# The convolution's first term on ScalarE, and eight weight tiles' low parts added by DMA, in a gated two-branch layer

## The chip, the cores and the metric

The kernel runs on one core of one Trainium2 chip. The time is the device time of one execution in microseconds (us); a kernel's time is the median of its runs. The profile is of one execution, taken apart from those runs.

The core has engines that run side by side, each with its own in-order queue of instructions: TensorE (PE in the profile; PEld is its weight load), VectorE (DVE), ScalarE (ACT), GpSimd (POOL) and SyncE (SP). Engines wait for one another by semaphores. Transfers (DMAs) are issued by an instruction on one of the queues, here SP's and POOL's, and then run on sixteen DMA engines; a DMA lands when its semaphore says that all its bytes are there.

## The reference

One layer over 512 tokens of 1024 channels. After an RMS norm, one projection makes the inputs of two branches and their gates. The memory branch (mLSTM, four heads of 256, computed in pairs of heads) takes its q and k through a causal convolution of width 4 per channel and a SiLU:

```python
h = rmsnorm(x, norm_w)
proj = jnp.einsum('bsd,de->bse', h, w_in) + b_in
...
qk = jax.nn.silu(causal_depthwise_conv(jnp.concatenate([mq, mk], axis=-1), conv_w, conv_b))
```

so that a channel's value at token t is the sum over j of conv_w[3 - j] x (its projection at t - j, bias included), plus conv_b. The other branch is a stick-breaking attention (eight heads of 128) without softmax. Both are projected, gated, added, sent through an output projection and added to x.

## The kernel before, in words

**Units.** All dense work is cut into units: a weight tile of 128 x 1024 numbers (512 KB), loaded by SP into `stg` (three buffers, tag shared), then split, then multiplied on TensorE. Each operand is held in two parts of the type fp32r, a high part (rounded, `wh`) and a low part (what the rounding left, `wl`), and a product takes three matmuls: high x high, high x low, low x high (`mm3`, L90 to L93). `split` (L95) makes the high part on ScalarE (L96) and the low part by a subtraction on VectorE (L97). A unit has 24 matmuls of 128 x 512, in two halves of twelve. Some units (those of `w_proj_m`, late in the kernel) are marked `by_dma`: there ScalarE makes wh (L123) and writes the same rounded tile with its sign turned into wl (L124), and POOL issues a DMA that adds the original tile from stg to it (L125).

**Order of the units.** Counted from 0: 0 to 15 are q, k, v and the gate of the attention's first four heads, 16 to 31 those of its second four; 32 to 51 are the first memory pair: output gate 32 to 35, gate 36 to 39, q 40 to 43, k 44 to 47, v 48 to 51; 52 to 71 are the second memory pair, with q in 64 to 67 and k in 68 to 71; then the merge gates (72 to 87), the two branch projections (88 to 95 and 96 to 103), and the output projection. The main loop (L1252) goes through the units: at step c it splits the tile of unit c + 2, evacuates unit c - 1 out of PSUM (`evac`), and computes unit c. wh and wl have three buffers each, the dense results four PSUM banks (`psd`); a unit of q, k or a gate takes one bank, and the four v units of a pair take four together, from the first of them on.

**Heads between the halves.** Between the two halves of a unit, each active head advances by one `yield`. The attention's heads 4 to 7 (`SbSet.head`, second set) start at steps 31, 34, 36 and 38. A head splits its q and k (`qtt`, `ktt`; the low parts on VectorE), has TensorE make scores, ScalarE two sigmoids of them (`om`, `a_all`), POOL the causal masks (L466, L469), VectorE the running products (L472, L473) and block transposes into `ay` (L490). Then sixteen DMAs of 40 KB move `ay` into `az` (L509), eight at one step and eight at the next; for these four heads POOL issues them. `az` has two buffers, used by the heads in turn, and a head's az is read in two goes: two pieces (`ath`), and two steps on the last piece (`at`), each split on ScalarE and VectorE.

**The convolution** (`MPair.qk_group`, L701) is the evacuation of the q and k units. ScalarE copies the bank into t and adds the projection's bias (L705); VectorE computes acc = t x w3 + conv_b (L708), then three times acc += t shifted x w (L710); ScalarE takes the sigmoid (L713). The rest of the SiLU (L716), the high part (L721) and the low part (L725) of a unit are interleaved with the next unit's evacuation by `self.prev`. acc has one buffer.

POOL's DMAs use eight semaphores in rotation; each waits for the previous transfer on its semaphore.

Of the kernel before, what the change touches and what calls it, by code (L numbers as in the profile page):

```python
# [11 lines left out]
AF = mybir.ActivationFunctionType  # L12
OP = mybir.AluOpType
# [22 lines left out]
def tile_hybrid_layer(  # L36
# [16 lines left out]
    nc = tc.nc  # L53
# [20 lines left out]
    def blk(tag, dt=F32, shape=(512,), name=None, p=128):  # L74

        where = mp if tag in MISC else sp
        return where.tile([p] + list(shape), dt, name=name or tag, tag=tag, bufs=BUFS[tag])

    def two(tag, dt=F32, name=None):

        t = blk(tag, dt, (2, 512), name=name)
        return t[:, 0, :], t[:, 1, :]

    def dense_ps():
        return psd.tile([128, 512], F32, name="dps", tag="dps")

    def att_ps():
        return psa.tile([128, 512], F32, name="aps", tag="aps")

    def mm3(ps, ah, al, bh, bl, first, last):  # L90
        nc.tensor.matmul(ps, ah, bh, start=first, stop=False)  # L91
        nc.tensor.matmul(ps, ah, bl, start=False, stop=False)  # L92
        nc.tensor.matmul(ps, al, bh, start=False, stop=last)  # L93
# [6 lines left out]
    class Unit:  # L100


        def __init__(self, src, c0, rows=None):
            if rows is None:
                self.ap = src[:, c0:c0 + 128].rearrange("(k p) c -> p k c", p=128)
                self.shape = [KT, 128]
            else:
                self.ap = src[rows:rows + 256, c0:c0 + 512].rearrange("(k p) c -> p k c", p=128)
                self.shape = [2, 512]
            self.slow = None  # L110
            self.heavy = False
            self.by_dma = False
# [16 lines left out]
    units = []  # L129

    def chan_group(src, c0, n, mov, evac, slow=None):
        for ct in range(n // 128):
            u = Unit(src, c0 + 128 * ct)

            def mm(half, u=u, ct=ct):
                if half == 0:
                    u.ps = dense_ps()
                for k in range(4 * half, 4 * half + 4):
                    mh, ml = mov(k)
                    mm3(u.ps, u.wh[:, k, :], u.wl[:, k, :], mh, ml, k == 0, k == KT - 1)  # L140

            u.mm = mm
            u.evac = lambda u=u, ct=ct: evac(ct, u.ps)
            u.slow = slow
            units.append(u)
# [50 lines left out]
    def defer(n, fn):  # L196
        later.setdefault(now[0] + n, []).append(fn)
# [24 lines left out]
    vec = cst.tile([128, 98], F32, name="vec")  # L222
    bvec = cst.tile([128, 56], F32, name="bvec")
# [23 lines left out]
    def turn_vecs():  # L247
        vp = att_ps()
        nc.tensor.transpose(vp[:, 0:98], v_rows, ident[0:98, 0:98])
        nc.tensor.transpose(vp[:, 98:154], b_rows, ident[0:56, 0:56])  # L250
        nc.vector.tensor_copy(vec, vp[:, 0:98])
        nc.vector.tensor_copy(bvec, vp[:, 98:154])
        nc.vector.scalar_tensor_tensor(qkw, vec[:, 96:97], 128 ** -0.5, vec[:, 97:98],
                                       op0=OP.mult, op1=OP.mult)

    def cw(j, ct):
        return vec[:, 8 + 16 * j + ct:9 + 16 * j + ct]

    def cb(ct):
        return vec[:, 72 + ct:73 + ct]  # L260
# [4 lines left out]
    def bias(ct):  # L265
        return bvec[:, ct:ct + 1]
# [51 lines left out]
    class SbSet:  # L318
# [95 lines left out]
        def v_group(self):  # L414
            row = []

            def evac(tb, ps):
                t = blk("tmp")
                nc.vector.tensor_tensor(t, ps, row[0], op=OP.add)
                vh = blk("vh", FR, (576,))[:, 0:512]  # L420
                vl = blk("vl", FR)
                nc.scalar.activation(vh, t, AF.Copy)
                self.v.append((vh, vl))
                if tb == TB - 1:
                    done.add(("v", self.s))
                return lambda: nc.vector.tensor_tensor(vl, t, vh.bitcast(F32), op=OP.subtract)

            tok_group(w_in, C_SV + 512 * self.s, h_sta, evac, False, C_SV + 512 * self.s, row)
# [246 lines left out]
    class MPair:  # L675
        def __init__(self, p):
            self.p = p
            self.prev = lambda: None
            self.tr = {"q": [], "k": []}
            self.v = []  # L680

# [19 lines left out]
        def qk_group(self, name, c0, o):  # L701
            def evac(ct, ps):
                ch = o + 4 * self.p + ct
                t = blk("tmp")
                nc.scalar.activation(t, ps, AF.Identity, bias=bias(ch))  # L705
                self.prev()
                acc = blk("acc")
                nc.vector.tensor_scalar(acc, t, cw(3, ch), cb(ch), op0=OP.mult, op1=OP.add)  # L708
                for j in (1, 2, 3):
                    nc.vector.scalar_tensor_tensor(acc[:, j:], t[:, 0:T - j], cw(3 - j, ch), acc[:, j:],  # L710
                                                   op0=OP.mult, op1=OP.add)
                self.prev()
                nc.scalar.activation(t, acc, AF.Sigmoid)  # L713

                def mult():
                    nc.vector.scalar_tensor_tensor(t, acc, 1.0 if name == "q" else 0.0625, t,  # L716
                                                   op0=OP.mult, op1=OP.mult)

                    def high():
                        th, tl = two("qk", FR, name="m%st" % name)  # L720
                        nc.scalar.activation(th, t, AF.Copy)  # L721
                        self.tr[name].append((th, tl))

                        def low():
                            nc.vector.tensor_tensor(tl, t, th.bitcast(F32), op=OP.subtract)  # L725
                            if ct == 3:
                                done.add(("m" + name, self.p))
                        self.prev = low
                    self.prev = high

                self.prev = mult
                if ct == 3 and name == "k":
                    def flush():
                        for _ in range(3):
                            self.prev()
                        self.prev = lambda: None
                    defer(1, flush)

            chan_group(w_in, c0 + 512 * self.p, 512, h_mov, evac, lambda: self.prev())

        def v_group(self):
            row = []
# [127 lines left out]
    pairs = [MPair(0), MPair(1)]  # L870
# [103 lines left out]

    chan_group(w_proj_m, 0, D, lambda k: ymp[k], pm_evac)
    n_proj = len(units)
    for un in units[n_proj - 8:]:
        un.by_dma = True


# [230 lines left out]
    for tb in range(TB):  # L1211
        units[tb].mm = first_mm(tb)

    later.setdefault(3, []).append(turn_vecs)
    later.setdefault(GATES_PREP, []).append(gates_prep)

# [102 lines left out]
```

## Time and profile before

| | us |
|---|---|
| Time, median of 3 runs | 705.88 (705.53 to 706.02) |
| The profiled execution's own time | 706.65 |
| Its span, first to last instruction | 704.9 |
| TensorE busy in it | 691.1 |
| VectorE, ScalarE, POOL busy | 472.4, 334.9, 166.0 |
| Units 40 to 47 on TensorE | 265.72 to 314.96 |
| Mean granted TensorE clock | 0.994 |

Rows of the timeline read: start, duration, engine, line, operation, written tile <- read tiles, shape, count, and in brackets the idle time just before and what ended it. Durations of neighbours on one engine overlap by a tenth or so in the rows: the spacing of starts is what an operation costs on its engine. Times are from the start of the span.

### The profile page before, as it was taken

How to read it: one execution, taken by the hardware profiler on the slowest of the kernel's cores; microseconds unless marked ns; L12 is line 12 of the kernel's file. 1: busy time of each engine (PE TensorE's matmuls, PEld its weight loads, DVE VectorE, ACT ScalarE, POOL GpSimd, SP SyncE). 2: the span in 40 equal slices, each digit the busy share in tenths (PEclk: the TensorE clock that was granted, in tenths of full speed). 3: DMA queues.
4: the chain of work that ended last, by engine and by line, in shares of the span. 5: the costliest groups of instructions: out<-in, count | busy, mean ns of one | idle time of the engine just before them, and what ended most of it. 6: DMA issues, size and time to landing. Idle time of an engine off the chain costs nothing.

```text
span 704.9 us, 9367 instructions
## 1 busy us (share of the span) xinstructions
PE 691.1 (98%) x3172; PEld 574.0 (81%) x3172; DVE 472.4 (67%) x835; ACT 334.9 (48%) x629; POOL 166.0 (24%) x361
## 2 busy tenths in 40 slices
PE   8999999999999999997999999999999999999997
PEld 6888788888888888885888888888888888888885
DVE  6847987866836897898634638995444364446995
ACT  6245364575335663444365634446463353344451
POOL 5422122265831686040002020001111000111010
PEclk9999999999999999998999999999999999999999
DMA  7423524525653443342332234433323456589344
GB/s 244 136 87 102 170 63 125 143 78 154 181 141 91 113 111 94 95 127 75 89 95 86 60 100 128 118 90 89 90 61 83 114 161 211 155 176 215 111 90 120
DMA packets 109113, 84.11 MB, mean 119 GB/s; under 512 B 8302, under 2 KB 91656, under 8 KB 109064
## 3 DMA queue, kind: packets, MB, share of 16 engines
q1 hardware_dynamic: 103320, 73.40, 36.4%
q0 software_dynamic: 5600, 9.97, 6.5%
q8 instruction: 25, 0.41, 0.2%
q14 instruction: 24, 0.20, 0.1%
q10 hardware_dynamic: 144, 0.13, 0.1%
HBM read 65.12 MB, written 2.10 MB: 95 GB/s over the span
## 4 chain that ended last, share of the span: by engine, by line
PE 59%; issue 12%; DVE 9%; DMA 6%; POOL 3%; ACT 1%; SPq 0%; DVEq 0%; POOLq 0%; ACTq 0%
PE dps L91 17%; PE dps L93 17%; PE dps L92 17%; DVE acc L710 2%; DMA wl<-stg 2%; POOL az L509 2%; PE aps L92 2%; PE aps L93 2%; PE aps L91 2%; DVE wl L97 1%; DMA az<-ay 1%; DMA xr<-u 1%; DMA stg<-in_w_proj_m_dram 1%; DMA xr<-in_x_dram 1%; DVE om L472 1%
## 5 line engine op out<-in xcount | busy, mean ns | idle before, releaser
L97 DVE TENSOR_TENSOR wl<-stg,wh 128x1024 fp32r<-128x1024 f32 x92 | 112.5, 1223 | 116.5 <-ACT wh L96 115.4
L91 PE MATMUL dps<-hh,wh 128*128 128x512 f32 x448 | 175.1, 391 | 0.0
L93 PE MATMUL dps<-hh,wl 128*128 128x512 f32 x448 | 174.5, 390 | 0.0
L92 PE MATMUL dps<-hl,wh 128*128 128x512 f32 x448 | 174.4, 389 | 0.0
L96 ACT ACTIVATE wh<-stg 128x1024 fp32r<-128x1024 f32 x92 | 96.8, 1052 | 64.5 <-PE dps L93 39.8
L93 PEld LDWEIGHTS dps<-hh,wl 128*128 128x128 f32 x448 | 84.1, 188 | 17.9
L92 PEld LDWEIGHTS dps<-hl,wh 128*128 128x128 f32 x448 | 84.2, 188 | 16.7
L91 PEld LDWEIGHTS dps<-hh,wh 128*128 128x128 f32 x448 | 84.2, 188 | 16.5
L91 PE MATMUL dps<-wh,hh 128*128 128x512 f32 x224 | 89.3, 399 | 4.8 <-ACT tmp L705 4.4
L93 PE MATMUL dps<-wh,hl 128*128 128x512 f32 x224 | 88.3, 394 | 0.0
L92 PE MATMUL dps<-wl,hh 128*128 128x512 f32 x224 | 88.2, 394 | 0.0
L91 PEld LDWEIGHTS dps<-wh,hh 128*128 128x128 f32 x224 | 42.8, 191 | 14.2 <-ACT tmp L705 4.8
L93 PEld LDWEIGHTS dps<-wh,hl 128*128 128x128 f32 x224 | 42.6, 190 | 9.2
L92 PEld LDWEIGHTS dps<-wl,hh 128*128 128x128 f32 x224 | 42.7, 191 | 8.4
L509 POOL DMA_DIRECT2D az<-ay x64 | 32.1, 508 | 25.0 <-DVE at L97 24.1
L713 ACT ACTIVATE tmp<-acc 128x512 f32<-128x512 f32 x16 | 10.1, 633 | 57.3 <-DVE acc L710 57.3
L710 DVE SCALAR_TENSOR_TENSOR acc<-tmp,vec,acc 128x511 f32<-128x511 f32 (+2 forms) x48 | 36.0, 750 | 1.7
L466 POOL TENSOR_SCALAR_AFFINE_SELECT om<-om 128x128 f32<-128x128 f32 x32 | 17.3, 541 | 80.0 <-ACT om L464 80.0
L472 DVE TENSOR_TENSOR_SCAN om<-om 128x512 f32<-128x512 f32 (+3 forms) x32 | 26.7, 834 | 8.6 <-POOL om L466 8.6
L125 POOL DMA_DIRECT2D wl<-stg x8 | 7.0, 870 | 93.7 <-DVE yml L97 61.7
L464 ACT ACTIVATE om<-aps,rq 128x512 f32<-128x512 f32 (+3 forms) x32 | 16.8, 526 | 21.6 <-PE aps L93 21.6
L399 POOL DMA_DIRECT2D tz<-ty x48 | 25.9, 549 | 5.0 <-DVE ty L389 2.4
(284 smaller groups left out, 1273.8 us busy)
## 6 DMA issues: line engine op xcount, KB each, us to landing
stg<-in_w_in_dram SPq DMA_DIRECT2D x87, 512.0 KB, 4.0
stg<-in_w_proj_s_dram SPq DMA_DIRECT2D x8, 512.0 KB, 3.9
B<-in_w_out_dram SPq DMA_DIRECT2D x8, 512.0 KB, 4.8
stg<-in_w_proj_m_dram SPq DMA_DIRECT2D x8, 512.0 KB, 3.7
wl<-stg POOLq DMA_DIRECT2D x8, 512.0 KB, 5.5
az<-ay SPq DMA_DIRECT2D x64, 40.0 KB, 2.7
az<-ay POOLq DMA_DIRECT2D x64, 40.0 KB, 2.0
brow<-in_b_in_dram SPq DMA_DIRECT2D x8, 256.0 KB, 5.5
```

What stands on the lines that cost most here:

```text
L91: nc.tensor.matmul(ps, ah, bh, start=first, stop=False)
L92: nc.tensor.matmul(ps, ah, bl, start=False, stop=False)
L93: nc.tensor.matmul(ps, al, bh, start=False, stop=last)
L96: nc.scalar.activation(hi, src, AF.Copy)
L97: nc.vector.tensor_tensor(lo, src, hi.bitcast(F32), op=OP.subtract)
L399: q.dma_start(tz[32 * b:32 * b + 32, :, a, :], src[32 * a:32 * a + 32, b])
L464: nc.scalar.activation(om[:, 0:n], zp, AF.Sigmoid, scale=rn[:, h:h + 1])
L466: nc.gpsimd.affine_select(out=om[:, ts], in_=om[:, ts], compare_op=OP.is_gt, fill=1.0, base=0, channel_multiplier=1, pattern=[[-1, 128]])
L472: nc.vector.tensor_tensor_scan(back, back, back, 1.0, op0=OP.mult, op1=OP.bypass)
L509: q.dma_start(az[32 * a:32 * a + 32, b, :, :], ay[32 * b:32 * b + 32, a, :, :])
L710: nc.vector.scalar_tensor_tensor(acc[:, j:], t[:, 0:T - j], cw(3 - j, ch), acc[:, j:], op0=OP.mult, op1=OP.add)
L713: nc.scalar.activation(t, acc, AF.Sigmoid)
```

## The change

Three things are done. The first term of the convolution, acc = t x w3 + conv_b on VectorE, becomes a second pass of ScalarE over the same PSUM bank, acc = ps x w3 + b'. As ps lacks the projection's bias, b' = w3 x bias + conv_b takes the place of conv_b; it is made once in the setup, by two small VectorE operations on 128 x 16 numbers; t and the other three terms stay as they were. And the eight q and k units of the first memory pair (40 to 47) are marked `by_dma`, as those of `w_proj_m` were before. Those of the second pair (64 to 71) get the new first term alone.

```diff
--- before.py
+++ after.py
@@ -250,6 +250,9 @@
         nc.tensor.transpose(vp[:, 98:154], b_rows, ident[0:56, 0:56])
         nc.vector.tensor_copy(vec, vp[:, 0:98])
         nc.vector.tensor_copy(bvec, vp[:, 98:154])
+
+        nc.vector.tensor_tensor(vp[:, 160:176], vec[:, 56:72], bvec[:, 0:16], op=OP.mult)
+        nc.vector.tensor_tensor(vec[:, 72:88], vp[:, 160:176], vec[:, 72:88], op=OP.add)
         nc.vector.scalar_tensor_tensor(qkw, vec[:, 96:97], 128 ** -0.5, vec[:, 97:98],
                                        op0=OP.mult, op1=OP.mult)
 
@@ -676,6 +679,7 @@
         def __init__(self, p):
             self.p = p
             self.prev = lambda: None
+            self.dense = []
             self.tr = {"q": [], "k": []}
             self.v = []
 
@@ -705,7 +709,7 @@
                 nc.scalar.activation(t, ps, AF.Identity, bias=bias(ch))
                 self.prev()
                 acc = blk("acc")
-                nc.vector.tensor_scalar(acc, t, cw(3, ch), cb(ch), op0=OP.mult, op1=OP.add)
+                nc.scalar.activation(acc, ps, AF.Identity, scale=cw(3, ch), bias=cb(ch))
                 for j in (1, 2, 3):
                     nc.vector.scalar_tensor_tensor(acc[:, j:], t[:, 0:T - j], cw(3 - j, ch), acc[:, j:],
                                                    op0=OP.mult, op1=OP.add)
@@ -737,6 +741,7 @@
                     defer(1, flush)
 
             chan_group(w_in, c0 + 512 * self.p, 512, h_mov, evac, lambda: self.prev())
+            self.dense.extend(units[-4:])
 
         def v_group(self):
             row = []
@@ -974,7 +979,7 @@
 
     chan_group(w_proj_m, 0, D, lambda k: ymp[k], pm_evac)
     n_proj = len(units)
-    for un in units[n_proj - 8:]:
+    for un in units[n_proj - 8:] + sum([p.dense for p in pairs[:1]], []):
         un.by_dma = True
```

In the changed kernel the lines are shifted: L705 becomes L709, L708 L712, L710 L714, L713 L717, L509 L512; L123 to L125 stay.

## The prediction

> **What bounds the kernel now.** I read the busy shares first, then what TensorE waited for, then the chain that ended last, then the four engines' timelines where that chain leaves TensorE.
>
> ```profile
> PE 691.1 (98%) x3172; PEld 574.0 (81%) x3172; DVE 472.4 (67%) x835; ACT 334.9 (48%) x629; POOL 166.0 (24%) x361
> PE dps L91 <- ACT tmp L705: 4.4, 1, 4.4
> PE aps L92 <- DVE ktt L97: 0.4, 1, 0.4
> 325.53 0.68 ACT tmp L705
> 326.25 0.79 PE dps L91
> ...
> 331.31 0.42 PE dps L93
> 331.73 0.24 PE dps L91
> 326.25 0.79 PE L91 MATMUL dps<-wh,hh 128*128 128x512 f32 x1 [4.42 <-ACT tmp L705]
> 291.24 0.39 PE L91 MATMUL dps<-hh,wh 128*128 128x512 f32 x1
> 296.68 0.39 PE L91 MATMUL dps<-hh,wh 128*128 128x512 f32 x1
> ```
>
> The first line has each engine's busy time; the next two are from the list of TensorE's waits (for whom: total, times, longest); then come pieces of the chain, and from TensorE's timeline the matmul behind the wait and the first ones of units 44 and 45. TensorE is busy all the time and sets the end. (Units are weight tiles, counted from 0; 40 to 43 are q and 44 to 47 are k of the first memory pair.) Its one long wait, 4.42 us before 326.25, is for L705: the four PSUM banks are full, and ScalarE is late emptying the one of unit 47. Behind the wait the matmuls start 0.43 apart instead of 0.227 (unit 44's 24 take 296.68 - 291.24 = 5.44): twelve take 326.25 to 331.73, 5.48 us, against 2.72, so 2.75 more. What can be won at TensorE here is 4.42 + 2.75 = 7.17 us.
>
> The lateness comes from VectorE's pace:
>
> ```profile
> 302.44 2.32 DVE L710 SCALAR_TENSOR_TENSOR acc<-tmp,vec,acc 128x511 f32<-128x511 f32 x3
> 306.47 1.22 DVE L97 TENSOR_TENSOR wl<-stg,wh 128x1024 fp32r<-128x1024 f32 x1 [0.26 <-ACT wh L96]
> 307.61 0.54 DVE L708 TENSOR_SCALAR acc<-tmp,vec 128x512 f32<-128x512 f32 x1
> 308.19 2.32 DVE L710 SCALAR_TENSOR_TENSOR acc<-tmp,vec,acc 128x511 f32<-128x511 f32 x3
> 304.85 0.63 ACT L713 ACTIVATE tmp<-acc 128x512 f32<-128x512 f32 x1 [3.38 <-DVE acc L710]
> 305.39 1.05 ACT L96 ACTIVATE wh<-stg 128x1024 fp32r<-128x1024 f32 x1
> 306.34 0.67 ACT L705 ACTIVATE tmp<-dps,bvec 128x512 f32<-128x512 f32 x1
> 306.91 0.62 ACT L721 ACTIVATE mqt<-tmp 128x512 fp32r<-128x512 f32 x1
> ```
>
> One round of the convolution (a unit's evacuation) takes 308.19 - 302.44 = 5.75 us, and VectorE has hardly a gap in it; a unit without head work takes 5.44 on TensorE, so each round falls behind a little, and rounds with a head's splits in them more. ScalarE, in the second half of the rows, waits 3.38 of each round for VectorE.
>
> **The change part by part.** It takes from VectorE, per unit of the first pair, the low part (1.14, from 306.47 to 307.61) and the first term (0.58). ScalarE gets them: a second 128x1024 copy (0.95) and a 128x512 pass from PSUM (0.57, as L705). A round becomes a loop through ScalarE: sigmoid 0.54, wh 0.95, wl 0.95, L705 0.57, high part 0.57, first term 0.57, handover 0.1, three VectorE terms and handover 2.41 (302.44 to 304.85): 6.66 us, 0.9 longer than now. So VectorE is relieved and the round isn't shorter. In the second pair, without the copy, it is 5.71, about today's pace: nothing there. The two small setup operations cost as this one, off the path:
>
> ```profile
> L252 DVE COPY bvec<-aps x1: 206/206/206, 36.5 to 36.5; 128x56 f32<-128x56 f32 x1
> ```
>
> That is 0.4 us at most (around 36.5 us, where TensorE's list names no wait for a low part), and I count 0.
>
> What decides is POOL's queue: the low part is now issued there, among the stick-breaking heads' copies az<-ay (heads 4 to 7, eight copies at a time). POOL, before, at units 38 and 39:
>
> ```order
> L509 DMA az_2731<-ay_2580 32x320 x8
> L465 MEMSET om_2750 128x1
> L466 AFFINE_SELECT om_2750<-om_2750 128x128
> L469 AFFINE_SELECT a_all_2664<-a_all_2664 128x128
> L465 MEMSET om_2760 128x1
> ```
>
> The same place after, with the semaphores waited for:
>
> ```order
> L125 DMA wl_2715<-stg_2558 128x1024 [waits DMASW0_49,DMAHW2_49,PE_49,Activation_49]
> L512 DMA az_2734<-ay_2582 32x320 [waits DMAHW4_49,DMAHW3_49,DMAHW5_49,DMAHW1_49,DMAHW6_49,DMAHW0_49,DMAHW7_49,DMASW1_49,DVE_49]
> L512 DMA az_2734<-ay_2582 32x320 [waits DMASW2_49]
> L512 DMA az_2734<-ay_2582 32x320 [waits DMASW3_49]
> L512 DMA az_2734<-ay_2582 32x320 [waits DMASW4_49]
> L512 DMA az_2734<-ay_2582 32x320 [waits DMASW5_49]
> L512 DMA az_2734<-ay_2582 32x320 [waits DMASW6_49]
> L512 DMA az_2734<-ay_2582 32x320 [waits DMASW7_49]
> L512 DMA az_2734<-ay_2582 32x320 [waits DMASW0_49]
> L468 MEMSET om_2753 128x1
> L469 AFFINE_SELECT om_2753<-om_2753 128x128 [waits Activation_49]
> ```
>
> A low part moved in ahead of the copies. Each DMA of POOL takes the next of eight semaphores and waits for that one's previous transfer. The low part has semaphore 0, so the eighth copy waits until the low part has landed; behind it stand the masks of head 7 (AFFINE_SELECT), behind those VectorE's scans, and behind these on VectorE the low parts qtt and ktt that the next scores need. Three units on, POOL before:
>
> ```order
> L465 MEMSET om_2938 128x1
> L466 AFFINE_SELECT om_2938<-om_2938 128x128
> L469 AFFINE_SELECT a_all_2832<-a_all_2832 128x128
> L509 DMA az_2909<-ay_2740 32x320 x8
> L509 DMA az_3058<-ay_2918 32x320 x16
> L751 MEMSET vh_3513 128x2
> ```
>
> and after:
>
> ```order
> L512 DMA az_2914<-ay_2743 32x320 x8
> L125 DMA wl_3034<-stg_2889 128x1024
> L512 DMA az_3065<-ay_2923 32x320 x8
> L125 DMA wl_3088<-stg_2970 128x1024
> L512 DMA az_3065<-ay_2923 32x320 x8
> L125 DMA wl_3158<-stg_3038 128x1024
> L125 DMA wl_3202<-stg_3092 128x1024
> ```
>
> wl_3034 is unit 44's low part and wl_3088 unit 45's, which now stands behind head 7's first eight copies. What these wait for, and the prices of the walk:
>
> ```profile
> 251.79 3.94 POOL L509 DMA_DIRECT2D az<-ay  x8 [0.36 <-DVE ay L490]
> 272.46 3.94 POOL L509 DMA_DIRECT2D az<-ay  x8 [6.57 <-DVE at L97]
> 299.38 6.55 POOL L509 DMA_DIRECT2D az<-ay  x13 [17.51 <-DVE at L97]
> 306.50 1.76 POOL L509 DMA_DIRECT2D az<-ay  x3 [0.57 <-DMA az<-ay]
> 298.52 0.56 DVE L97 TENSOR_TENSOR at<-az,at 128x384 fp32r<-128x384 f32 x1 [0.57 <-ACT at L96]
> 253.01 1.05 ACT L96 ACTIVATE wh<-stg 128x1024 fp32r<-128x1024 f32 x1
> 618.42 1.04 ACT L124 ACTIVATE wl<-stg 128x1024 fp32r<-128x1024 f32 x1
> 619.75 0.86 POOL L125 DMA_DIRECT2D wl<-stg  x1 [4.57 <-ACT wl L124]
> DMA to landing us min/median/max: 4.6/5.5/8.2
> 257.73 0.65 DVE L472 TENSOR_TENSOR_SCAN om<-om 128x256 f32<-128x256 f32 x1
> 261.70 0.50 PE L92 MATMUL aps<-ktt,qtt 128*128 128x512 f32 x1 [0.37 <-DVE ktt L97]
> 265.72 0.39 PE L91 MATMUL dps<-hh,wh 128*128 128x512 f32 x1
> 276.78 0.76 DVE L472 TENSOR_TENSOR_SCAN om<-om 128x256 f32<-128x256 f32 x1 [3.62 <-POOL om L466]
> 279.61 1.22 DVE L97 TENSOR_TENSOR wl<-stg,wh 128x1024 fp32r<-128x1024 f32 x1
> 284.56 0.39 PE L91 MATMUL dps<-hh,wh 128*128 128x512 f32 x1
> 297.99 0.51 ACT L96 ACTIVATE at<-az 128x384 fp32r<-128x384 f32 x1
> 298.40 1.03 ACT L96 ACTIVATE ath<-az 128x512 fp32r<-128x512 f32 x2
> ```
>
> Head 7's copies start at 299.38, 0.3 after head 5's last split (298.52 + 0.56) frees the two-buffer tile az; head 6's wait likewise (272.46). They issue eight in 3.94. The landing row is of the eight low parts that are made by DMA today, late in the kernel.
>
> The walk, from these durations. (a) Unit 40: wl on ScalarE from 253.96, POOL issues at 255.3 (0.29 after its end, as 618.42 to 619.75), landing at 255.3 + 5.5 = 260.8; the eighth copy 0.49, its mask 0.38 (276.78 - 272.46 - 3.94): first scan at 261.7, not 257.73. From that scan to the scoring matmul that waits for ktt are 3.97 today: 265.65, 3.95 later than 261.70. The idle of 0.37 + 3.95 = 4.3 is as long as the 4.42 above, so I add its 2.75 of clock; unit 40 starts at 272.4.
> (b) ScalarE then empties unit 39 (0.6), makes wh and wl (1.9) and head 4's piece (0.41, 297.99 to 298.40): 275.3; VectorE's split 0.65, POOL 0.3: copies from 276.3. Unit 42's low part, issued at 275.2, lands at 280.7; with the last copy and mask 281.6. Scans as from 276.78 to 279.61, 2.83: the three terms of unit 40 start at 284.4, its sigmoid 2.41 later at 286.8.
> (c) Two rounds, 6.66 + 1.03 (ath) and 6.66: sigmoid of unit 42 at 301.15; it takes 0.54, head 5's piece 0.41, VectorE 0.65, POOL 0.3: head 7's copies at 303.05; eight of them, 3.94: unit 45's low part is issued at 307.0 and lands at 312.5.
> (d) TensorE reaches unit 45 at 272.4 + (296.68 - 265.72) = 303.4 and its third matmul, the first with wl, 0.45 later. It waits 8.7, and the clock costs 2.75 again; unit 45 ends at 312.5 + 22 x 0.227 + 2.75 = 320.3. The low parts of 40 to 44 come in time (44, the closest, at 296.1 for 298.3); that of 46, behind eight more copies and the landing of 45, comes at 318.5, before 320.3.
> (e) Rounds 43 and 44 end at about 316, before unit 45 does, so the lag is gone by then. The first term keeps a bank 1.14 longer (high part and its own pass), which matters only where banks are short, at unit 48, and not without the lag. So the old wait goes, with its clock: 7.17.
> (f) SP's loads into stg now wait for a landing in place of VectorE. That of unit 48 starts at 312.5 and takes the page's 4.0 us, to 316.5; ScalarE can split it only when unit 45 frees its wh, at 320.3. It is hidden, by 3.8 (the row, and those on the landing, stand here):
>
> ```profile
> stg<-in_w_in_dram SPq DMA_DIRECT2D x87, 512.0 KB, 4.0
> 250.00:300.00 50.00, 49.63 (x227) 41.23 (x226) 43.28 (x81) 24.01 (x43) 24.07 (x57) 1.00 0.36 101
> 600.00:650.00 50.00, 50.00 (x222) 41.41 (x221) 25.38 (x38) 20.79 (x24) 6.96 (x8) 1.00 0.78 183
> q0 software_dynamic: 1054, 3.86, 42.1%
> ```
>
> Sum: 3.95 + 2.75 + 8.7 + 2.75 - 7.17 = +11.0. The profiled execution took 706.65 (span 704.9), 0.77 above the median 705.88: 717.65, or 716.9 on the median's scale. Differences under 0.2% (1.4 us) I call none.
>
> Two prices have no row at this place. The landing has 4.6 to 8.2 late in the kernel; I take its 5.5, because the traffic will be alike: the DMA share is 0.36 in 250 to 300 and 0.78 in 600 to 650 (the number before the last), where POOL's own eight low parts are 42.1% of the queues' time, and 0.36 + 0.42 = 0.78. Three landings lie on the path (units 40, 42, 45): -2.7 if all take 4.6, +5.4 if two take 8.2. The clock after (a) is bounded by 0 (the wait of 0.37 was followed by no halving) and 2.75; I take the near row. [...]
>
> **The rivals.**
> Forecast (74%): waits as walked; with those bounds 711.5 to 722.3.
> Least wait (12%): (a) doesn't reach TensorE and nothing runs late. Even so, from unit 42's end to unit 45's landing are 6.12 (the loop without its sigmoid) + 0.54 + 0.41 + 0.65 + 0.3 + 3.94 + 5.5 = 17.5, against 296.68 - 284.56 + 0.45 = 12.6 until the need: 4.9 + 2.75 - 7.17 = +0.5, 706.4. That is no measurable change. Against it: VectorE waits for POOL's masks even today (3.62 at 276.78).
> Faster (14%): head 7's copies wait only for their own transposes, and POOL comes to unit 45 at once. It decides at a landing by 297.1, an issue by 291.6. Then only relief is left: -7.17, 698.7. For it: VectorE loses 1.7 of 5.75 per unit. Against it: the 17.51 row, and the order.
>
> **How the numbers follow.** 716.9 is the likeliest. 706 to 722.5 takes in the forecast's bounds and the least wait, and leaves out the faster case and about 0.06 at the forecast's ends. Least wait counts mostly as none: faster 0.14, same 0.08, slower 0.78.
>
> **What would show it.** Right: PE waits for ktt (about 4 us near 262) and for a DMA wl at unit 45 (about 9), each with a halved clock; the L705 wait gone; VectorE's share down, gaps before its scans. Wrong: no PE wait for wl, or POOL issuing unit 45's low part before 292.

## The result, and the profile after

| | before | after |
|---|---|---|
| Median (lowest to highest) | 705.95 us (705.53 to 706.37), 4 runs | 714.54 us (714.12 to 715.41), 4 runs |
| The profiled execution's own time, its span | 706.65, 704.9 | 714.22, 712.5 |

The ratio is 1.0123, with a 95% interval from 1.0106 to 1.0141: 8.6 us slower. The busy times of the engines, and the head of the list of TensorE's waits, after:

```profile
PE 690.1 (97%) x3172; PEld 573.2 (80%) x3172; DVE 456.7 (64%) x813; ACT 353.2 (50%) x653; POOL 170.7 (24%) x369
```

```profile
PE dps L93 <- DMA wl<-stg: 8.7, 1, 8.7
PE aps L92 <- DVE ktt L97: 4.3, 1, 4.3
```

The change did what it says: VectorE has 15.7 us less, ScalarE 18.3 more. The old wait for L705 isn't in the list any more; in its place stand two, one for a low part that a DMA makes and one for ktt. POOL's timeline shows where both come from:

```profile
254.60 0.94 POOL L125 DMA_DIRECT2D wl<-stg  x1 [3.91 <-ACT wl L124]
255.41 3.59 POOL L512 DMA_DIRECT2D az<-ay  x7
259.77 0.50 POOL L512 DMA_DIRECT2D az<-ay  x1 [0.76 <-DMA wl<-stg]
...
303.00 3.95 POOL L512 DMA_DIRECT2D az<-ay  x8 [11.69 <-DVE at L97]
306.91 0.98 POOL L125 DMA_DIRECT2D wl<-stg  x1
```

The first row is unit 40's low part. The first seven copies stand behind it, so they start at 255.41 where they started at 251.79 before; the eighth waits 0.76 more for its landing. (Row times count from the start of each span. Unit 36 starts 0.71 us sooner in this execution than in the one before, so on a common clock the seven copies are 4.33 late.) The last two rows are head 7's copies, held 11.69 us for the end of head 5's splits, and behind them unit 45's low part. VectorE, with the scan that needs the mask and the first convolution terms of unit 40:

```profile
260.64 0.84 DVE L475 TENSOR_TENSOR_SCAN om<-om 128x256 f32<-128x256 f32 x1 [4.80 <-POOL om L469]
...
264.14 0.69 DVE L97 TENSOR_TENSOR ktt<-tz,ktt 128x512 fp32r<-128x512 f32 x1
...
284.21 2.31 DVE L714 SCALAR_TENSOR_TENSOR acc<-tmp,vec,acc 128x511 f32<-128x511 f32 x3
```

ScalarE's sigmoids of units 40 to 42, and its wait before them, which ends with VectorE's terms:

```profile
286.62 0.63 ACT L717 ACTIVATE tmp<-acc 128x512 f32<-128x512 f32 x1 [4.75 <-DVE acc L714]
...
294.32 0.64 ACT L717 ACTIVATE tmp<-acc 128x512 f32<-128x512 f32 x1 [2.45 <-DVE acc L714]
...
301.06 0.63 ACT L717 ACTIVATE tmp<-acc 128x512 f32<-128x512 f32 x1 [2.45 <-DVE acc L714]
```

And TensorE at the two waits (302.39 is unit 45's first matmul, 311.74 the first that needs its wl):

```profile
264.89 0.79 PE L92 MATMUL aps<-ktt,qtt 128*128 128x512 f32 x1 [4.27 <-DVE ktt L97]
...
302.39 0.39 PE L91 MATMUL dps<-hh,wh 128*128 128x512 f32 x1
302.61 0.39 PE L92 MATMUL dps<-hl,wh 128*128 128x512 f32 x1
311.74 0.80 PE L93 MATMUL dps<-hh,wl 128*128 128x512 f32 x1 [8.74 <-DMA wl<-stg]
312.34 0.63 PE L91 MATMUL dps<-hh,wh 128*128 128x512 f32 x1
...
314.47 0.50 PE L93 MATMUL dps<-hh,wl 128*128 128x512 f32 x1
314.81 0.39 PE L91 MATMUL dps<-hh,wh 128*128 128x512 f32 x1
```

To compare kernels, this table gives where units start on TensorE, in us after unit 36, whose surroundings are alike in all of them; then where unit 36 itself starts, and how long the rest from unit 104 to the end of the span takes. All are starts of first matmuls in the timelines of the profiled executions.

| kernel | 40 | 45 | 46 | 48 | 50 | 104 | unit 36 at | 104 to end |
|---|---|---|---|---|---|---|---|---|
| before | 26.33 | 57.29 | 62.73 | 75.57 | 96.30 | 421.61 | 239.39 | 43.90 |
| after | 32.72 | 63.71 | 79.53 | 92.41 | 105.25 | 430.56 | 238.68 | 43.26 |
| term_only | 26.33 | 57.29 | 62.73 | 75.57 | 95.07 | 420.38 | 240.65 | 43.97 |
| dma_only | 32.74 | 63.70 | 79.59 | 92.70 | 105.54 | 430.85 | 238.67 | 43.48 |
| own_az | 31.82 | 62.79 | 68.23 | 82.57 | 102.32 | 427.63 | 239.12 | 42.65 |
| from_42 | 26.31 | 57.27 | 73.05 | 85.91 | 98.75 | 424.08 | 238.81 | 47.51 |
| both_mends | 26.30 | 57.26 | 62.70 | 77.16 | 95.64 | 421.16 | 238.58 | 46.16 |
| tiny_dma | 26.31 | 57.27 | 62.71 | 77.21 | 95.52 | 420.83 | 239.49 | 42.78 |
| act_load | 26.34 | 57.30 | 62.74 | 75.91 | 97.84 | 423.57 | 238.88 | 43.95 |
| shadow_before | 26.30 | 57.25 | 62.69 | 76.64 | 90.36 | 415.66 | 238.87 | 43.87 |
| shadow_term | 26.32 | 57.28 | 63.18 | 79.67 | 95.39 | 420.77 | 239.04 | 43.99 |
| shadow_after | 32.43 | 64.91 | 78.79 | 92.12 | 104.96 | 430.54 | 238.37 | 43.09 |
| shadow_dma | 26.35 | 58.97 | 65.48 | 80.57 | 93.41 | 418.72 | 238.34 | 42.74 |

After, TensorE loses 32.72 - 26.33 = 6.39 at unit 40 and (79.53 - 63.71) - (62.73 - 57.29) = 10.38 at unit 45, and wins (96.30 - 75.57) - (105.25 - 92.41) = 7.89 at unit 48. From unit 50 to unit 104 both kernels take 325.31, so nothing more happens there.

### The profile page after: what moved, and what is told of

It reads as the page before. It is cut to its first block, busy times and chain, and to the rows that moved or that the text cites. A ratio compares the mean times of both kernels' runs of the same rounds, so it can differ in the third digit from the quotient of the medians.

```text
span 712.5 us, 9379 instructions
## 1 busy us (share of the span) xinstructions
PE 690.1 (97%) x3172; PEld 573.2 (80%) x3172; DVE 456.7 (64%) x813; ACT 353.2 (50%) x653; POOL 170.7 (24%) x369
## 4 chain that ended last, share of the span: by engine, by line
PE 79%; DMA 4%; DVE 3%; issue 2%; ACT 2%; POOL 1%; SPq 0%; DVEq 0%; ACTq 0%; POOLq 0%
PE dps L91 23%; PE dps L93 23%; PE dps L92 23%; PE aps L92 3%; PE aps L93 3%; PE aps L91 3%; DMA wl<-stg 2%; DMA az<-ay 1%; PE aps L823 1%; PE aps L825 1%; PE aps L824 1%; DVE acc L714 1%; DMA stg<-in_w_in_dram 1%; POOL az L512 1%; SPq L512 0%
## 5 line engine op out<-in xcount | busy, mean ns | idle before, releaser
L97 DVE TENSOR_TENSOR wl<-stg,wh 128x1024 fp32r<-128x1024 f32 x84 | 102.6, 1222 | 120.3 <-ACT wh L96 119.2
L96 ACT ACTIVATE wh<-stg 128x1024 fp32r<-128x1024 f32 x84 | 88.4, 1053 | 66.5 <-PE dps L93 41.6
L714 DVE SCALAR_TENSOR_TENSOR acc<-tmp,vec,acc 128x511 f32<-128x511 f32 (+2 forms) x48 | 36.0, 750 | 15.4 <-ACT acc L712 14.3
L125 POOL DMA_DIRECT2D wl<-stg x16 | 14.3, 916 | 106.2 <-DVE yml L97 61.7
L512 POOL DMA_DIRECT2D az<-ay x64 | 32.8, 638 | 16.0 <-DVE at L97 11.7
L469 POOL TENSOR_SCALAR_AFFINE_SELECT om<-om 128x128 f32<-128x128 f32 x32 | 15.8, 494 | 79.4 <-ACT om L467 79.4
L717 ACT ACTIVATE tmp<-acc 128x512 f32<-128x512 f32 x16 | 10.1, 633 | 41.5 <-DVE acc L714 41.5
L123 ACT ACTIVATE wh<-stg 128x1024 fp32r<-128x1024 f32 x16 | 16.9, 1055 | 26.8 <-PE dps L92 20.4
L467 ACT ACTIVATE om<-aps,rq 128x512 f32<-128x512 f32 (+3 forms) x32 | 16.8, 525 | 23.4 <-PE aps L93 23.3
```

The costliest lines, as they stand in the source:

```text
L96: nc.scalar.activation(hi, src, AF.Copy)
L97: nc.vector.tensor_tensor(lo, src, hi.bitcast(F32), op=OP.subtract)
L123: nc.scalar.activation(self.wh, self.st, AF.Copy)
L125: nc.gpsimd.dma_start(out=self.wl, in_=self.st, accum_op=OP.add)
L467: nc.scalar.activation(om[:, 0:n], zp, AF.Sigmoid, scale=rn[:, h:h + 1])
L469: nc.gpsimd.affine_select(out=om[:, ts], in_=om[:, ts], compare_op=OP.is_gt, fill=1.0, base=0, channel_multiplier=1, pattern=[[-1, 128]])
```

## The experiments

My theory was the prediction's: POOL's queue, in two places that are independent of each other. The rivals were that one of the two parts of the change costs by itself what it puts on ScalarE, and that the waits only move.

**The first term alone** (term_only). The changed kernel without the marks:

```diff
-    for un in units[n_proj - 8:] + sum([p.dense for p in pairs[:1]], []):
+    for un in units[n_proj - 8:]:
```

> The changed kernel with the low parts of units 40 to 47 back on VectorE: only the first term of the convolution moves to ScalarE. Theory (the loss comes from POOL's queue): both new waits of TensorE, for ktt and for unit 45's low part, are gone; a round of the convolution is a loop through ScalarE of 5.7 us, so VectorE's relief of 0.58 counts only in the three rounds that also hold a head's splits, about 1.7 us; 704.2, with a rest of the wait for a bank at unit 48. Rival (the loss comes from ScalarE's added passes in the round): slower than before, about 708.

Measured: 705.26 us, ratio 0.9998 (0.9988 to 1.0007) to the kernel before. TensorE's longest wait:

```profile
PE dps L91 <- ACT acc L712: 4.5, 2, 4.1
```

No change that can be measured, where I had expected 704.2; the bank wait at unit 48 stays and is now ended by the new pass L712. In this execution unit 50 comes 1.2 us sooner (95.07 for 96.30), but the wait itself is only 0.29 shorter (4.13 for 4.42). The rest is TensorE's clock, which stood at half for 3.42 us of the work behind the wait in place of 5.34 (see point (d) below on how that comes about).

**The low parts alone** (dma_only): the first term back on VectorE, the marks kept.

```diff
-                nc.scalar.activation(acc, ps, AF.Identity, scale=cw(3, ch), bias=cb(ch))
+                nc.vector.tensor_scalar(acc, t, cw(3, ch), cb(ch), op0=OP.mult, op1=OP.add)
```

(and the two setup operations that fold the bias are taken out).

> The changed kernel with the first term back on VectorE: only the low parts of units 40 to 47 go by DMA. Theory (POOL's queue): nearly the whole loss stays; the wait for ktt (about 4 us and its clock) as it is, the wait at unit 45 about 1 us shorter, since a round has one ScalarE pass and the high part less in its loop (6.1 for 6.7): 713.4. Rival (ScalarE's added passes): half of the loss, about 710.

Measured: 714.77 us, 1.0125 (1.0105 to 1.0146), with waits of 8.8 for the DMA and 4.2 for ktt. The whole loss lies in the low parts; the first term doesn't add to it. I had expected a wait 1 us shorter at unit 45, and it isn't: head 7's copies go out 0.7 us sooner (302.31) and the low part 0.4 sooner (306.47), but this one takes 5.2 us to land, for 4.8.

**Head 7's copies in other buffers** (own_az): the changed kernel, where head 7's az comes from a tag of four buffers, so its copies need not wait for head 5's splits.

```diff
-            az = sp.tile([128, 4, 10, 32], F32, name="az", tag="P5", bufs=2)
+            last = self.s and h == 3
+            az = sp.tile([128, 4, 10, 32], F32, name="az", tag="A" if last else "P5", bufs=4 if last else 2)
```

> The changed kernel, but head 7's az is taken from the four-buffer tag A, so that its copies need not wait until head 5's last split has freed the two-buffer tag P5. Nothing else is moved. Theory (unit 45's low part stands behind copies that wait): TensorE's wait of 8.7 us at unit 45 is gone. But the rounds, now 6.7 us, are late all the same, and TensorE no longer stands still for them: the old wait for a bank at unit 48 is back with 4 to 5 us and its clock. The two nearly cancel: about 712. Rival (the DMA itself is too slow, or the sixteen DMA engines too full): the wait at unit 45 stays, 714.5.

Measured: 710.78 us, 1.0076 (1.0059 to 1.0093). POOL's rows for head 7's first copies and unit 45's low part, and TensorE's waits:

```profile
290.44 3.78 POOL L513 DMA_DIRECT2D az<-ay  x7
...
296.61 0.92 POOL L125 DMA_DIRECT2D wl<-stg  x1 [1.12 <-ACT wl L124]
```

```profile
PE aps L92 <- DVE ktt L97: 4.3, 1, 4.3
PE dps L91 <- ACT acc L713: 3.8, 1, 3.8
PE dps L93 <- DMA wl<-stg: 1.2, 1, 1.2
```

The copies go out 12.6 us sooner, the low part 10.3 sooner, and the wait of 8.7 falls to 1.2. At once the bank wait at unit 48 is back. So the second wait is the copies' wait for az, and part of what it costs in the changed kernel is offset by the old wait that it hides.

**Units 40 and 41 split as before** (from_42):

```diff
-    for un in units[n_proj - 8:] + sum([p.dense for p in pairs[:1]], []):
+    for un in units[n_proj - 8:] + pairs[0].dense[2:]:
```

> The changed kernel, but units 40 and 41 are split by VectorE; 42 to 47 go by DMA. Theory: no low part stands ahead of the copies and masks of steps 38 and 39, so the wait for ktt and its clock (6.4 us) are gone. Unit 45's low part still waits for head 5's last split, and TensorE reaches unit 45 6.4 us sooner while that split comes about 3 us sooner, so that wait grows to about 12: about 712. Rival (each low part by DMA costs about the same, 1.1 us of the 8.6 for each of eight): 712.4 too, but with both waits shortened in proportion instead of one gone and one longer.

Measured: 712.44 us, 1.0097 (1.0082 to 1.0112). POOL's rows:

```profile
251.20 3.93 POOL L512 DMA_DIRECT2D az<-ay  x8 [0.37 <-DVE ay L493]
...
296.66 3.95 POOL L512 DMA_DIRECT2D az<-ay  x8 [11.69 <-DVE at L97]
300.59 0.97 POOL L125 DMA_DIRECT2D wl<-stg  x1
...
687.63 1.77 POOL L1092 DMA_DIRECT2D xr<-u  x2 [13.78 <-DVE wl L97]
```

The eight copies of the first row start as in the kernel before, and the wait for ktt is gone: unit 40 starts at 26.31, as before the change. The wait at unit 45 stays, 8.7; I had thought that it would grow to 12. It doesn't, because head 7's copies too go out 6.34 us sooner (296.66 for 303.00), by as much as TensorE reaches unit 45 sooner (57.27 for 63.71), and not 3. In the stretch this kernel is only 98.75 - 96.30 = 2.45 late, yet its median is 6.9 above. Most of the rest is at the other end of the kernel (47.51 us from unit 104, for 43.90), and the last row belongs to it: an accumulating DMA of the output projection waits for a VectorE operation later than its source u, and later TensorE waits 1.8 for the wl of the last unit. The kernel before, at the same place, and then the changed kernel one pair of these DMAs earlier:

```profile
682.79 1.75 POOL L1087 DMA_DIRECT2D xr<-u  x2 [10.86 <-DVE u L1104]
```

```profile
681.36 1.75 POOL L1092 DMA_DIRECT2D xr<-u  x2 [25.25 <-DVE wl L97]
```

Such a wait stands in the changed kernel too, at the first pair, and its end is no longer than before (43.26). So the wait alone doesn't make the end longer; where it falls matters.

**Both mends** (both_mends): the two edits above together.

> The changed kernel with units 40 and 41 split by VectorE as before and with head 7's copies in buffers of their own; units 42 to 47 still get their low parts by accumulating DMA. Theory (the loss is two waits of POOL's queue, each with a place of its own): no wait for ktt above 0.5 us, a wait of at most 3 us for a low part at unit 45 (it was 1.2 with the own buffers alone), the bank wait at unit 48 back at 3.5 to 7 us; unit 50 starts 0 to 2 us later after unit 36 than in the kernel before; 706 to 708 us, plus the 3.5 us at the end of the kernel that the run with units 40 and 41 alone changed showed, should it come from the number of POOL's DMAs, which is the same here. Rival (the 0.95 us more of ScalarE's work per unit is what costs): the stretch is no shorter than with either mend alone, unit 50 is 5 us or more late, 711 us or more.

Measured: 707.89 us (705.78 to 709.48), 1.0036 (1.0023 to 1.0048). In the stretch unit 50 is 0.66 earlier than before the change, with waits of 3.7 for a bank and 1.3 for a low part. The two losses are independent: counted at unit 50, the own buffers alone win 2.93, the split of units 40 and 41 alone 6.50, and both together 9.61, about the sum of the two and more than the 8.95 that the change loses there. The longer end is there again, 46.16.

**Two small DMAs** (tiny_dma): both mends, and for units 40 and 41 a DMA of 512 bytes where the changed kernel issues the low part.

```diff
                 split(self.st, self.wh, self.wl)
+                if self in pairs[0].dense[:2]:
+                    nc.gpsimd.dma_start(out=sp.tile([128, 1], F32, name="nul", tag="nul", bufs=1), in_=vec[:, 0:1])
```

> Both mends, and on POOL, in the places where the changed kernel issues the low parts of units 40 and 41, a DMA of 512 bytes each into a tile that nothing reads: as many POOL DMAs as the changed kernel has, each on the same one of the eight semaphores. Theory (the eighth copy of head 5 waits for the landing of what holds its semaphore, and what matters is that 512 KB land late; the longer end of the kernel with six DMAs more comes from the semaphores that its last DMAs then get): no wait for ktt above 0.6 us; no wait for wl at unit 107; 42.6 to 44.0 us from unit 104 to the end in place of 46.2 and 47.5; 704 to 706 us. Rival (the longer end has another cause): it stays at 46 us or more, 707.9 us.

Measured: 704.16 us (702.67 to 704.80, 7 runs), 0.9975 (0.9964 to 0.9986). POOL:

```profile
251.49 0.57 POOL L129 DMA_DIRECT2D nul<-vec  x1
252.06 3.94 POOL L515 DMA_DIRECT2D az<-ay  x8
...
682.51 1.77 POOL L1095 DMA_DIRECT2D xr<-u  x2 [8.30 <-DVE u L1112]
```

The DMA ahead of the copies costs TensorE nothing here: it has no wait before it, it takes POOL 0.57 us, the eight copies behind it take 3.94 as before, and unit 40 starts at 26.31. And the end is 42.78 again. With 0 or 8 POOL DMAs more than before it took 42.65 to 43.99 in all kernels of the table, with 6 more 46.16 and 47.51. As POOL's DMAs take eight semaphores in turn, the number of DMAs ahead, modulo eight, sets which semaphores the last ones get, and that fits these three counts; other counts were not run. Why it makes one of the last DMAs wait for a later VectorE operation stays open.

**ScalarE's work without POOL's** (act_load): the changed kernel, but for units 40 to 47 VectorE writes the low part over what ScalarE's extra pass wrote, and POOL issues nothing.

```diff
-                nc.gpsimd.dma_start(out=self.wl, in_=self.st, accum_op=OP.add)
+                if self in pairs[0].dense:
+                    nc.vector.tensor_tensor(self.wl, self.st, self.wh.bitcast(F32), op=OP.subtract)
+                else:
+                    nc.gpsimd.dma_start(out=self.wl, in_=self.st, accum_op=OP.add)
```

> The changed kernel in which ScalarE still writes the extra pass over the low part for units 40 to 47, and VectorE then writes the low part over it, so POOL issues no DMA for them. Theory (POOL's queue and the landing are the loss, not ScalarE's time): no wait of PE for a DMA or for ktt above 0.5 us; rounds of 6.5 to 6.8 us, so the bank wait at unit 48 is 5 to 8 us in place of 4.4; 706 to 709 us. Rival (ScalarE's longer rounds are the loss): 712 us or more, with waits of PE for wl from VectorE.

Measured: 707.81 us, 1.0037 (1.0025 to 1.0048). TensorE's waits:

```profile
PE dps L91 <- ACT acc L715: 5.1, 2, 4.1
...
PE aps L91 <- ACT at L96: 1.1, 1, 1.1
```

Neither of the two new waits is there, though a round takes 6.74 us as in the changed kernel (sigmoids at 305.13 and 311.87). So ScalarE's extra pass costs 2.0 us by the medians here, where VectorE still makes the low parts after it; the other 6.6 of the 8.6 come only with POOL's DMAs. The 2.0 need not be a share of the 8.6: in both_mends the rounds of units 42 to 47 are as long (6.74), and its stretch is no longer than before the change.

**Another order on ScalarE** (shadow_before, shadow_term). What would help here? In the kernel before, ScalarE makes the next wh after the sigmoid, and VectorE's next low part waits for that wh (0.26 us in the prediction's row at 306.47). In shadow_before nothing of the change is done; the split is only called earlier, so that ScalarE makes wh while VectorE adds the convolution's terms:

```diff
                                                    op0=OP.mult, op1=OP.add)
+                ahead(now[0])
                 self.prev()
                 nc.scalar.activation(t, acc, AF.Sigmoid)
...
             units[c - 1].slow()
-            ahead(c)
```

shadow_term has the first term on ScalarE as well.

> The kernel before, with the high part of the unit after next made by ScalarE while VectorE adds the convolution's terms of the current unit, ahead of the sigmoid, not after it. Theory (the rounds of heads 6 and 7 are a chain through ScalarE and VectorE, in which ScalarE's passes over the weights stand in series with the convolution): the round falls from 5.75 to 5.1 to 5.4 us, the bank wait at unit 48 falls from 4.4 to 1 to 2.5 us, 700 to 704 us. Rival (the round is VectorE's busy time): the round stays at 5.7 us, 705.6 us.

> The same new order with the convolution's first term on ScalarE, low parts by VectorE. Theory: VectorE is then the longer of the two in a round, with 0.6 us less; round 4.5 to 4.9 us, no bank wait above 0.5 us, so the 4.4 us and the slow-clocked work after it go: 697 to 700 us. Rival (the chain is not what holds the bank): 705 us, as with the first term alone.

Measured: shadow_before 700.28 us (699.85 to 700.33, 5 runs), 0.9927 (0.9914 to 0.9939), 5.5 us faster than the kernel before. shadow_term 706.15 us (11 runs), 1.0005 (0.9996 to 1.0014). VectorE in the rounds of units 44 and 45 of shadow_before:

```profile
304.96 2.32 DVE L710 SCALAR_TENSOR_TENSOR acc<-tmp,vec,acc 128x511 f32<-128x511 f32 x3
307.20 1.22 DVE L97 TENSOR_TENSOR wl<-stg,wh 128x1024 fp32r<-128x1024 f32 x1
...
310.44 2.32 DVE L710 SCALAR_TENSOR_TENSOR acc<-tmp,vec,acc 128x511 f32<-128x511 f32 x3
```

and of shadow_term:

```profile
307.17 2.32 DVE L714 SCALAR_TENSOR_TENSOR acc<-tmp,vec,acc 128x511 f32<-128x511 f32 x3 [1.40 <-ACT acc L712]
...
313.24 2.32 DVE L714 SCALAR_TENSOR_TENSOR acc<-tmp,vec,acc 128x511 f32<-128x511 f32 x3 [1.41 <-ACT acc L712]
```

A round without head work takes 5.48 in the first, a little more than I had thought, and the wait of 4.4 falls to 0.6, and the granted clock stays at 1.00 from 300 to 330 us. In the second it takes 6.07: VectorE stands 1.4 us in every round for ScalarE's pass, whose work was to relieve it, and TensorE waits 2.5 for a bank and 1.8 for a wl. I had taken the first term off VectorE and forgotten to put it into the chain, against the prediction's own reading that the round becomes a loop through ScalarE.

**The new order with the DMAs** (shadow_after, shadow_dma). The first is the changed kernel with the two edits of that order; the second is tiny_dma with them and with the first term back on VectorE.

> The changed kernel with ScalarE's passes over the weights ahead of the sigmoid, as in the two runs of that order; POOL's queue has the same order as in the changed kernel. Theory (POOL's queue sets both waits, whatever ScalarE's order): PE waits 4 us for ktt and 6 us or more for the low part of unit 45; 712 to 718 us. Rival (a shorter round lets the copies and so the low part go early enough): the wait at unit 45 falls below 3 us, 706 us or less.

> The faster order (first term on VectorE, ScalarE's passes ahead of the sigmoid) with the change's low parts by DMA for units 42 to 47, head 7's copies in their own buffers, and the two 512-byte DMAs. Theory: VectorE, which bounds that order's round of 5.48 us, loses 1.14 us a round less what then shows of the sigmoid, so the round falls to 4.8 to 5.2 us, but PE has only 1.4 us of waits left there to win, and the low part of unit 45 may still come 1 us late: 699.0 to 701.5 us. Rival (ScalarE, 1 us longer a round, takes over): the round is 5.6 us or more and PE waits 3 us or more: 703 us or more.

Measured: shadow_after 713.60 us, 1.0115 (1.0101 to 1.0129), shadow_dma 701.58 us, 0.9943 (0.9931 to 0.9956). TensorE's waits, first of shadow_after, then of shadow_dma:

```profile
PE dps L93 <- DMA wl<-stg: 8.1, 3, 6.7
PE aps L92 <- DVE ktt L97: 4.3, 1, 4.3
```

```profile
PE dps L93 <- DMA wl<-stg: 4.1, 3, 2.0
```

ScalarE's order doesn't cure POOL's queue: both waits stay in shadow_after. In shadow_dma both places are mended, and VectorE is relieved in the order in which its work fills nearly the whole round. There the round falls to 4.46 (terms at 296.32 and 300.78), more than I had expected, but TensorE waits 4.1 us for late low parts in place of shadow_before's 1.4 for wl and bank. By the two intervals neither of the two is ahead for certain; the DMA low parts bring nothing that can be measured even there. shadow_before, which moves one call and changes nothing else, is the fastest kernel of this study by its median.

## Why the prediction was right, point by point

**(a) Unit 40.** Right: the wait is 4.27 for 4.3, the first scan at 260.64 for 261.7, and unit 40 is 6.39 late for 6.70. The from_42 run shows that the DMA of units 40 and 41 is the cause, and act_load that ScalarE's pass without the DMA isn't. One thing in it the prediction told in the wrong proportion: it spoke of the eighth copy's wait for the landing, which is only 0.76. Most of the lateness is that POOL waits 3.91 for ScalarE's wl pass with seven copies queued behind it. The walk had both in its times. No run takes away one of the two and leaves the other: the two DMAs of tiny_dma have neither.

**(b), (c) The rounds and head 7.** Right: terms of unit 40 at 284.21 (284.4), its sigmoid at 286.62 (286.8), that of unit 42 at 301.06 (301.15), a round of 301.06 - 294.32 = 6.74 (6.66), head 7's copies at 303.00 (303.05), unit 45's low part issued at 306.91 (307.0). That they agree so closely is partly luck: this execution started 0.71 us ahead (unit 36), and counted from unit 36 these times are 0.5 to 0.7 late. Of the three landings on the path two were shorter than the 5.5 taken (4.9 for unit 40, 4.8 for unit 45) and one a little longer (5.7 for unit 42). The issues of L125 from 250 to 330 us, and the windows row of 250 to 300 us:

```profile
DMA to landing us min/median/max: 4.4/4.8/7.9
```

```profile
250.00:300.00 50.00, 45.73 (x199) 37.92 (x198) 31.61 (x65) 28.35 (x45) 25.23 (x59) 0.93 0.61 142
```

The DMA share rose to 0.61, not to the 0.78 that the choice of 5.5 rested on.

**(d) Unit 45.** The wait is 8.74 for 8.7: need and landing were both about 0.8 early, most of it the 0.71 above. The clock was the mis-sized term. I had 2.75 again; the slow spacing of 0.43 ends by 314.81, 3.07 after the wait (5.3 in the kernel before), and the whole delay is 10.38 for 11.45, so 1.5 to 1.7 was paid. The windows of this stretch show why (first TensorE's busy time; the granted clock is the third number from the end):

```profile
304.45:307.86 3.41, 0.00 (x0) 0.00 (x0) 1.10 (x2) 2.24 (x4) 3.41 (x8) 1.00 0.30 84
307.86:311.27 3.41, 0.00 (x0) 0.00 (x0) 2.45 (x4) 2.13 (x3) 3.41 (x8) 0.50 0.87 172
311.27:314.69 3.42, 2.95 (x7) 2.38 (x8) 1.20 (x2) 2.16 (x4) 2.50 (x5) 0.50 0.73 215
314.69:318.10 3.41, 3.41 (x16) 2.83 (x16) 2.35 (x4) 0.63 (x1) 0.00 (x0) 1.00 1.10 229
```

The clock was at half from 307.86 to 314.69, 6.83 us, and more than half of that passed while TensorE stood still anyway. Only 2.95 us of work ran at half (the granted clock of 0.50 in the rows), which costs 1.48 by an estimate of half that time. In the kernel before, the clock was at half from 324.76 to 331.59, as long, but the wait ended at 326.25, so 5.34 us of work ran at half. What counts is how much of the slow stretch lies behind the wait, and the walk had no term for that. The 1.5 to 1.7 is no fixed price either: at unit 40, 5.42 us of work ran at half (264.89 to 270.31).

**(e) The old wait.** Gone, worth 7.89 for 7.17. Of the 0.7 more, 0.16 is the counting of idle time from a modelled end and 0.2 a wait for at that went too; the rest I can't place. That the old wait comes back as soon as the new one is shorter is shown by own_az (3.8) and both_mends (3.7).

**(f)** Right: no wait for a load in TensorE's list.

Sum: the stretch gave 6.39 + 10.38 - 7.89 and small change, +8.95 by unit 104, for +11.0. The three terms were off by 0.31, 1.07 and 0.72, all to the same side; half of it is the clock at unit 45. The profiled span grew by 7.6, as this execution's start was 0.71 shorter and its end 0.64: unit 36 starts anywhere from 238.34 to 240.65 in the table. By the medians it was 8.6. Of the rivals, the faster case failed at the point that it named: the issue came at 306.91, not by 291.6. The least wait failed at (a).

## What to carry to other kernels

Before a piece of work is moved to an engine with time to spare, list what is queued behind it there and what it must wait for: POOL was 24% busy, and the two waits that come from low parts issued there cost 16.8 us with their clock, more than the 7.9 that the change won. A wait that vanishes may only be covered by a new, longer one, so mend one at a time and look whether the old one comes back. And a pass that is taken off a busy engine brings little if it comes back into the same chain on another: here the order of the passes was worth 5.5 us and their place nothing.

## What the runs showed of the hardware that was not expected

- How long TensorE works at the half clock (granted 0.50) after a wait doesn't follow the length of the wait. It was 2.95 us after 8.74 us of waiting and 5.42 after 4.27 (after), 5.34 after 4.42 (before), 3.42 after 4.13 (term_only) and 6.06 after 3.79 (own_az). In shadow_term a wait of 1.77 was followed by 3.41 at half, which began 1.12 after the wait had ended, and one of 2.55 by none. In the traces of before and after, all changes of the granted clock from 20 us to the end of the span, between 1.00 and 0.50, lie whole multiples of 3.413 us apart: 324.76, 331.59 and 703.64 before (2 and 109 of them), 263.49, 270.31, 307.86, 314.69 and 710.63 after (2, 11, 2 and 116). In these two kernels, cut at these times into stretches of that length, each stretch with the clock full that the half clock followed had TensorE idle for 2.70 us or more (2.93 and 3.41 before, 2.87, 3.41 and 2.70 after), and no other for more than 1.45 (301.03 to 304.45 after). Two stretches of that length, of shadow_term with 1.77 us idle and of act_load with 1.75, and what followed:

```profile
302.32:305.74 3.42, 1.65 (x8) 1.03 (x7) 3.38 (x5) 1.11 (x2) 2.84 (x6) 1.00 0.37 77
305.74:309.15 3.41, 3.41 (x13) 2.83 (x11) 1.94 (x4) 2.34 (x4) 1.18 (x4) 0.50 0.60 196
```

```profile
321.98:325.39 3.41, 1.66 (x6) 1.05 (x6) 3.11 (x6) 0.96 (x3) 0.00 (x0) 1.00 0.62 151
325.39:328.81 3.42, 0.62 (x3) 0.53 (x4) 2.89 (x4) 2.75 (x5) 0.00 (x0) 1.00 0.04 5
```

  After the first the granted clock was 0.50, after the second 1.00. These idle times rest on modelled ends of matmuls, so 0.02 us between two of them places no line, and no run here shifts a wait against such times to see what follows. As a price, 0 to 3.0 us per wait is an estimate from these runs: half of the time worked at the half clock, 0 to 6.06 us.
- Six DMAs more on POOL's queue, between 268 and 307 us, came with a longer end of the kernel, 46.16 us (both_mends) and 47.51 (from_42) from unit 104 on for 43.90 before; with two idle DMAs of 512 bytes besides (tiny_dma) it took 42.78.
